# Hybrid GLA / RG-LRU block on one core: output weights split beside the attention, second gate on the results

## The chip, the cores and the metric

The kernel runs on one NeuronCore of a Trainium2 chip. The engines are named as the profile names them: PE (TensorE, matmuls), DVE (VectorE), ACT (ScalarE), POOL (GpSimd), SP (SyncE, which issues most of the DMA transfers; POOL issues some). The metric is the time of one execution on the device, in microseconds; less is better.

## What is computed

The reference takes 1024 latent tokens and 256 context tokens of width 1024 (1280 rows, ten tiles of 128) through two layers. Layer 0 has gated linear attention with four heads and, beside it, a short gated convolution; layer 1 has a gated linear recurrence in both directions. Cut to what matters here:

```python
# layer 0 (x and the context alike)
h = rmsnorm(x) * (1 + scale) + shift
q, k, v, g_a, a_f, a_b, c_b, c_c, c_x, g_b = split(h @ w_in)
o = rmsnorm(gla_fwd(q, k, v, a_f) + gla_bwd(q, k, v, a_b)) * silu(g_a)
y = c_b * conv3(c_c * c_x) * silu(g_b)
x = x + gate0 * (concat(o, y) @ w_out0)        # w_out0: 2048 x 1024
# layer 1
h = rmsnorm(x) * (1 + scale1) + shift1
y = (rglru_fwd(h @ w_x) + rglru_bwd(h @ w_x)) * silu(h @ w_g)
x = x + gate1 * (y @ w_out1)                   # w_out1: 2048 x 1024
return rmsnorm(x) * final_g
```

`gate0` and `gate1` are rows of 1024 numbers, one for each column of the result.

## The kernel before

All is float32, and the matmuls keep that precision by parts: each operand is split into a rounded part `hi` and a rest `lo`, and `mm3` (L125 to L127) makes three matmuls of a product, hi x hi, hi x lo and lo x hi. Activations of a layer stand split in `hhi` and `hlo`. A weight tile is 128 x 512 numbers, 256 KB. `load_split` (L106 to L112) brings one in: a transfer on SP's queue into one of two `raw` buffers, a cast to `hi` on ACT (L111), and a subtraction for `lo` on DVE (L112), into one of six `hl` buffers that all weights share. A unit of projection weights is two such tiles (1024 x 128 weights) and gives PE 72 matmuls, 24 products over columns 256, 512 and 512.

Layer 0 goes head by head. For each of four heads `emit_gla` is written first, the attention proper: small float32 matmuls (`pz`, `psc`, `pk`, `pst`, `po`, `pot`) that hang on long chains over ACT and DVE. Then come two gate units (`wgt`), the conv channel's units `cc`, `cx`, `cb` and its gate unit, and then q, k and v of the next head. Their projections need nothing but their weights, and the scheduler of the framework mixes the attention's matmuls in between them; it decides each engine's order when the program is built, and on the chip each engine keeps it.

Between these units stands `presplit` (L166): layer 1's input weights are split while layer 0 runs. One call for one tile is a load into `raw` (L106), cast, subtraction, and two stores of 256 KB each (L173) into `w1s_d` in DRAM, all on SP's queue. There are 80 tiles, five at each of four points of a head. In layer 1 `load_parts` (L178) brings both parts back with one transfer of 512 KB on POOL's queue, with no cast.

The output projections are `out_group` (L632). Layer 0's runs over three groups of row tiles (3, 3 and 4 tiles), layer 1's over two of 4. Each group loops over 16 slices k of the inner dimension and two halves j of the columns, and every (k, j) needs one tile of the output weight: 32 tiles a group, 96 loads in layer 0 and 64 in layer 1, each by `load_split` (`rawo`, `wo`). The gated activations y come by SP's queue as well. The products of the last two slices are held back and done row tile by row tile. What the results are multiplied with differs: layer 0 and layer 1's first group multiply the results in PSUM by the gate row and add the residual; layer 1's second group has the gate in its weights (`gate=gb1`, one more DVE operation for each tile, L110) and only adds the residual (L978).

POOL has little to do besides the transfers of parts: the powers of the norms, `rr` (L90), one for each row tile.

## Time and profile before

| | us |
|---|---|
| median of 3 runs | 1995.36 (1992.71 to 1997.35) |
| the profiled execution | 2002.68 |
| its span on the core | 2000.9 |
| PE busy in the span | 1932.0 |
| DVE, ACT, POOL busy | 1317.8, 961.3, 105.2 |

In the span, the four heads of layer 0's attention take about 90 to 783 us, the other conv channels go on to about 960, layer 0's output projection runs from 985 to about 1272, the recurrence of layer 1 follows, and layer 1's output projection ends the kernel from about 1780. Engine names with a q (SPq) are that engine's queue of instructions. The view of busy time by stretch has, for each stretch in us from the span's start, its length, the busy time of each engine with its number of instructions, the granted share of PE's clock (1.00 is 2.4 GHz), the busy share of the 16 transfer engines, and GB/s. The view of one tile gives for each line, engine and operation the count, the shortest, median and longest duration in ns, and the first and last start in us. The timeline gives start and duration in us, and in brackets how long the engine was idle and what released it.

### The profile page before, as it was taken

What the parts mean: (1) busy time and instruction counts of PE and PEld (TensorE: products, weight loads), DVE (VectorE), ACT (ScalarE), POOL (GpSimd) and SP (SyncE); (2) the same over time, 40 slices, a digit from 0 to 9 for tenths busy, and PEclk for the clock granted to TensorE, in tenths of its full rate; (3) what the DMA queues carried; (4) which work ended last, traced back from release to release, by engine and by line L of the source; (5) the groups of instructions that cost most, each with busy time, mean ns of one, the idle gap of its engine ahead of it and who ended that gap; (6) DMA issues with size and microseconds to landing.
All of it is one profiled execution on the core that took longest, in us unless ns stands there. A gap on an engine that the chain in (4) does not pass through costs nothing.

```text
span 2000.9 us, 27096 instructions
## 1 busy us (share of the span) xinstructions
PE 1932.0 (97%) x9884; PEld 1588.5 (79%) x9884; DVE 1317.8 (66%) x2103; ACT 961.3 (48%) x1690; POOL 105.2 (5%) x154
## 2 busy tenths in 40 slices
PE   9899999999999999999999899999999999998988
PEld 5777898888788888888776678878888888876767
DVE  6746436543552554388557474689999999996595
ACT  4333344334433433311345444267777776876452
POOL 1000000000000000000000000201111010100000
PEclk9999999999999999999999999999999999999999
DMA  9256217514721751366655665434333343324782
GB/s 357 82 195 199 78 50 252 175 43 146 244 89 33 245 192 53 124 223 197 205 175 178 209 222 173 139 111 127 120 118 120 115 121 121 116 81 156 264 290 88
DMA packets 162522, 311.45 MB, mean 156 GB/s; under 512 B 16338, under 2 KB 37202, under 8 KB 162260
## 3 DMA queue, kind: packets, MB, share of 16 engines
q1 hardware_dynamic: 140628, 267.78, 40.1%
q0 software_dynamic: 21760, 41.95, 7.5%
q8 instruction: 77, 1.26, 0.3%
q14 instruction: 57, 0.47, 0.1%
HBM read 221.05 MB, written 88.60 MB: 155 GB/s over the span
## 4 chain that ended last, share of the span: by engine, by line
PE 60%; DMA 19%; DVE 12%; ACT 5%; issue 4%; SPq 1%; POOL 0%; DVEq 0%; ACTq 0%; POOLq 0%
PE pjgt L126 4%; PE pjgt L127 4%; PE pjgt L125 4%; DMA rawpre<-in_w1f 4%; PE pjxr L125 4%; PE pjxr L127 4%; PE pjxr L126 4%; PE pO L126 3%; PE pO L125 3%; PE pO L127 3%; PE po L515 2%; DMA wt<-in_wmT 2%; DMA rawo<-in_w0out 2%; PE pv L125 2%; PE pv L126 2%
## 5 line engine op out<-in xcount | busy, mean ns | idle before, releaser
L125 PE MATMUL pjgt<-hhi,wgt 128*128 128x512 f32 (+1 forms) x640 | 240.6, 376 | 6.0 <-DVE zc L218 6.0
L125 PE MATMUL pO<-wo,yh 128*128 128x512 f32 x576 | 224.2, 405 | 17.6 <-ACT wo L111 16.6
L126 PE MATMUL pjgt<-hlo,wgt 128*128 128x512 f32 (+1 forms) x640 | 240.5, 376 | 0.0
L127 PE MATMUL pjgt<-hhi,wgt 128*128 128x512 f32 (+1 forms) x640 | 239.5, 376 | 0.0
L126 PE MATMUL pO<-wo,yh 128*128 128x512 f32 x576 | 231.1, 402 | 7.2 <-DVE wo L112 7.2
L127 PE MATMUL pO<-wo,yl 128*128 128x512 f32 x576 | 228.5, 399 | 0.0
L806 DVE SCALAR_TENSOR_TENSOR xc<-xp,col,xc 128x1283 f32<-128x1283 f32 (+2 forms) x102 | 149.8, 1476 | 3.2
L111 ACT CAST wo<-rawo 128x512 fp32r<-128x512 f32 x160 | 98.0, 619 | 110.7 <-DMA rawo<-in_w0out 74.9
L112 DVE TENSOR_TENSOR wo<-rawo,wo 128x512 fp32r<-128x512 f32 x160 | 108.5, 687 | 63.6 <-ACT wo L111 63.0
L125 PEld LDWEIGHTS pO<-wo,yh 128*128 128x128 f32 x576 | 109.3, 191 | 50.0 <-ACT wo L111 22.5
L125 PEld LDWEIGHTS pjgt<-hhi,wgt 128*128 128x128 f32 x640 | 121.0, 189 | 30.1 <-DVE zc L218 6.6
L126 PEld LDWEIGHTS pjgt<-hlo,wgt 128*128 128x128 f32 x640 | 121.1, 189 | 23.7 <-issue 1.1
L127 PEld LDWEIGHTS pjgt<-hhi,wgt 128*128 128x128 f32 x640 | 120.5, 189 | 23.4 <-issue 0.7
L126 PEld LDWEIGHTS pO<-wo,yh 128*128 128x128 f32 x576 | 109.7, 190 | 36.8 <-DVE wo L112 12.4
L125 PE MATMUL pjxr<-hhi,wxr 128*128 128x512 f32 (+1 forms) x384 | 137.4, 359 | 0.0
L126 PE MATMUL pjxr<-hlo,wxr 128*128 128x512 f32 (+1 forms) x384 | 137.1, 358 | 0.0
L127 PE MATMUL pjxr<-hhi,wxr 128*128 128x512 f32 (+1 forms) x384 | 136.8, 358 | 0.0
L127 PEld LDWEIGHTS pO<-wo,yl 128*128 128x128 f32 x576 | 109.8, 191 | 24.6 <-DVE yl L685 0.3
L112 DVE TENSOR_TENSOR wpre<-rawpre,wpre 128x512 fp32r<-128x512 f32 x80 | 55.1, 690 | 90.1 <-ACT wpre L111 89.7
L125 PE MATMUL pv<-wv,hhi 128*128 128x256 f32 (+1 forms) x320 | 91.8, 287 | 2.4 <-ACT v L387 2.4
L127 PE MATMUL pv<-wv,hlo 128*128 128x256 f32 (+1 forms) x320 | 92.9, 290 | 0.0
L126 PE MATMUL pv<-wv,hhi 128*128 128x256 f32 (+1 forms) x320 | 92.8, 290 | 0.0
(270 smaller groups left out, 4527.9 us busy)
## 6 DMA issues: line engine op xcount, KB each, us to landing
w1s_d<-wpre SPq DMA_DIRECT2D x160, 256.0 KB, 2.6
rawo<-in_w0out SPq DMA_DIRECT2D x96, 256.0 KB, 3.2
rawpre<-in_w1f SPq DMA_DIRECT2D x64, 256.0 KB, 3.1
wt<-in_wmT SPq DMA_DIRECT2D x32, 512.0 KB, 4.3
rawo<-in_w1out SPq DMA_DIRECT2D x64, 256.0 KB, 3.3
wxr<-w1s_d POOLq DMA_DIRECT2D x32, 512.0 KB, 3.8
wgt<-w1s_d POOLq DMA_DIRECT2D x32, 512.0 KB, 3.8
wm<-in_wmT SPq DMA_DIRECT2D x24, 512.0 KB, 8.1
```

Source lines behind the costliest of these rows:

```text
L111: S.copy(hi, raw)
L112: V.tensor_tensor(lo, raw, hi.bitcast(F32), ALU.subtract)
L125: PE.matmul(ps, a[0], b[0], start=first, stop=False)
L126: PE.matmul(ps, a[0], b[1], start=False, stop=False)
L127: PE.matmul(ps, a[1], b[0], start=False, stop=last)
L515: PE.matmul(ps[:, :DV], l, r, start=(i == 0), stop=(i == len(pairs) - 1))
L806: V.scalar_tensor_tensor(x, tap(j), cw[j], x, op0=ALU.mult, op1=ALU.add)
```

## The change

It does three things. The 64 tiles of both output weights (32 each) are put at the head of the list that `presplit` works through, and each of the four points of a head takes nine tiles instead of five. Their parts go to `wos_d`, one such tensor for each layer. `out_group` and `load_w1` then load parts: one transfer of 512 KB on POOL's queue for each tile, straight into an `hl` buffer (6 of them, or 8 of its own pool in layer 1's second group), no cast, no subtraction. And since these parts have no gate in them, layer 1's second group multiplies its results by the gate row as the first one does.

```diff
-    todo = [(b, j) for b in range(NB) for j in range(5)]
+    wos_d = [dram.tile([32, P, 2, 512], F32, name=f"wos{l}_d") for l in range(2)]
+    todo = [(l, k, j, None) for l in range(2) for k in range(16) for j in range(2)]
+    todo += [(b, j) for b in range(NB) for j in range(5)]
...
-            b, j = todo.pop(0)
+            b, j, *o = todo.pop(0)
+            if o:
+                hi, lo = load_split((w0out, w1out)[b][j, :, 512 * o[0]:512 * o[0] + 512], 512,
+                                    f"preo{b}_{j}_{o[0]}", queue=SY.dma_start)
+                for i, part in enumerate((hi, lo)):
+                    SY.dma_start(wos_d[b][2 * j + o[0]][:, i], part.bitcast(F32))
+                continue
...
                 emit_raw_gate(w0f[8 + 2 * h], 2 * h)
-                presplit(5)
+                presplit(9)
                 emit_raw_gate(w0f[9 + 2 * h], 2 * h + 1)
-                presplit(5)
+                presplit(9)
                 for _ in emit_conv(h):
-                    presplit(5)
+                    presplit(9)
...
         def load_w(k, j):
+            if parts is not None:
+                pool, n = (wkw["pool"], 8) if wkw else (wpool, 6)
+                hl = pool.tile([P, 2, 512 if n == 8 else UW], F32R, tag="hl", bufs=n, name=f"wo{name}{g0}_{k}_{j}")
+                G.dma_start(hl[:, :, :512], parts[2 * k + j])
+                return hl[:, 0, :512], hl[:, 1, :512]
...
-            w1[k, j] = load_split(w1out[k, :, j * 512:(j + 1) * 512], 512, f"o10_{k}_{j}")
+            hl = wpool.tile([P, 2, UW], F32R, tag="hl", bufs=6, name=f"wo10_{k}_{j}")[:, :, :512]
+            G.dma_start(hl, wos_d[1][2 * k + j])
+            w1[k, j] = hl[:, 0], hl[:, 1]
...
-                                                 gate=gb1, late_k=3, pool=op, bufs=(4, 8), width=512)
+                                                 late_k=3, pool=op, parts=wos_d[1])
...
-                    if g0:
-                        V.tensor_tensor(x2[:, fs], acc[i][j], xr[:, fs], ALU.add)
-                    else:
-                        V.tensor_tensor(x2[:, fs], acc[i][j], gb1[:, fs], ALU.mult)
-                        V.tensor_tensor(x2[:, fs], x2[:, fs], xr[:, fs], ALU.add)
+                    V.tensor_tensor(x2[:, fs], acc[i][j], gb1[:, fs], ALU.mult)
+                    V.tensor_tensor(x2[:, fs], x2[:, fs], xr[:, fs], ALU.add)
```

How the order of instructions moves. On SP's queue, in the second head, between the last load for `cx` and the loads for `cb`, there stood before five pre-splits (`rawpre` is a load, `w1s_d<-wpre` the two stores of one):

```order
L97 DMA rawcx_0_1_3869<-in_w0f 128x512
L106 DMA rawpre_0_3957<-in_w1f 128x512
L106 DMA rawpre_1_3964<-in_w1f 128x512
L173 DMA w1s_d<-wpre_0_3959 128x512 x2
L106 DMA rawpre_2_3971<-in_w1ax 128x512
L173 DMA w1s_d<-wpre_1_3966 128x512 x2
L106 DMA rawpre_3_3978<-in_w1f 128x512
L173 DMA w1s_d<-wpre_2_3973 128x512 x2
L106 DMA rawpre_4_3985<-in_w1f 128x512
L173 DMA w1s_d<-wpre_3_3980 128x512 x2
L97 DMA rawcb_0_0_3992<-in_w0f 128x512
```

Now nine stand there, all of layer 1's output weight; these are the last five of them (`rawpreo` is a load, `wos_d<-wpreo` the two stores of one):

```order
L106 DMA rawpreo_13_0_4155<-in_w1out 128x512
L176 DMA wos_d<-wpreo_12_1_4150 128x512 x2
L106 DMA rawpreo_13_1_4162<-in_w1out 128x512
L176 DMA wos_d<-wpreo_13_0_4157 128x512 x2
L106 DMA rawpreo_14_0_4169<-in_w1out 128x512
L176 DMA wos_d<-wpreo_13_1_4164 128x512 x2
L106 DMA rawpreo_14_1_4176<-in_w1out 128x512
L176 DMA wos_d<-wpreo_14_0_4171 128x512 x2
L106 DMA rawpreo_15_0_4183<-in_w1out 128x512
L176 DMA wos_d<-wpreo_14_1_4178 128x512 x2
L97 DMA rawcb_0_0_4190<-in_w0f 128x512
```

The load for `cb` has moved behind four more loads and eight more stores; the same holds at each of the four points of each head.

On PE, in the same head, the rows just ahead of the first product with `cc`'s weights were, before, the end of the second gate unit (`pjgt`) and the attention's transposes and scores of the first of the two 512-row chunks that the backward pass takes (`pk`, `psc`, named 768):

```order
L465 MATMUL pk_1_768_3038<-ident,k_1_1_768_3024 128x128 x4
L488 MATMUL psc_1_6_3044<-qh_1_768_3022,kh_1_768_3023 64x128
L489 MATMUL psc_1_6_3044<-qh_1_768_3022,kh_1_768_3023 64x64
L127 MATMUL pjgt_768_3711<-hhi,wgt_0_1_3652 128x512
L125 MATMUL pjgt_768_3711<-hhi,wgt_0_1_3652 128x512
L126 MATMUL pjgt_768_3711<-hlo,wgt_0_1_3652 128x512
L127 MATMUL pjgt_768_3711<-hhi,wgt_0_1_3652 128x512
L125 MATMUL pjcc_0_3786<-hhi,wcc_0_0_3778 128x256
```

Now the scores of the next chunk (named 256) stand there as well, and the state products `pst` of the first chunk lie ahead of them:

```order
L497 MATMUL psc_1_2_3228<-qh_1_256_3206,kh_1_256_3207 64x128
L498 MATMUL psc_1_2_3228<-qh_1_256_3206,kh_1_256_3207 64x64
L497 MATMUL psc_1_2_3228<-qh_1_256_3206,kh_1_256_3207 64x128
L498 MATMUL psc_1_2_3228<-qh_1_256_3206,kh_1_256_3207 64x64
L497 MATMUL psc_1_2_3228<-qh_1_256_3206,kh_1_256_3207 64x128
L498 MATMUL psc_1_2_3228<-qh_1_256_3206,kh_1_256_3207 64x64
L497 MATMUL psc_1_2_3228<-qh_1_256_3206,kh_1_256_3207 64x128
L498 MATMUL psc_1_2_3228<-qh_1_256_3206,kh_1_256_3207 64x64
L474 MATMUL pk_1_256_3222<-ident,k_1_1_256_3208 128x128 x4
L125 MATMUL pjcc_0_3956<-hhi,wcc_0_0_3948 128x256
```

From the head's first gate product to this place, the attention's matmuls have grown from 12 psc, 6 pk, 2 pst and 1 pz to 20, 10, 6 and 2; up to the conv channel's gate unit from 20 psc, 10 pk, 9 pst, 3 pz and no po or pot to 32, 16, 13, 4, 12 and 6.

On POOL's queue, at the end of layer 0's first group of row tiles, only the powers of the norms stood before:

```order
L90 TENSOR_TENSOR rro_9_6981<-rvo_9_6979,m_77 128x1
L90 TENSOR_TENSOR rr_0_10051<-rv_0_10049,m_77 128x1
L90 TENSOR_TENSOR rr_1_10065<-rv_1_10063,m_77 128x1
L90 TENSOR_TENSOR rr_2_10080<-rv_2_10078,m_77 128x1
L90 TENSOR_TENSOR rr_3_10880<-rv_3_10878,m_77 128x1
```

Now the loads of the next group's weights stand ahead of them, each of which waits for a free `hl` buffer:

```order
L654 DMA wo_15_0_10277<-wos_d 128x2x512
L654 DMA wo_15_1_10279<-wos_d 128x2x512
L654 DMA wo_0_0_10549<-wos_d 128x2x512
L654 DMA wo_0_1_10560<-wos_d 128x2x512
L654 DMA wo_1_0_10581<-wos_d 128x2x512
L90 TENSOR_TENSOR rr_0_10405<-rv_0_10403,m_77 128x1
L90 TENSOR_TENSOR rr_1_10419<-rv_1_10417,m_77 128x1
L654 DMA wo_1_1_10592<-wos_d 128x2x512
L654 DMA wo_2_0_10613<-wos_d 128x2x512
L654 DMA wo_2_1_10624<-wos_d 128x2x512
L90 TENSOR_TENSOR rr_2_10434<-rv_2_10432,m_77 128x1
```

The powers of a group's rows have moved behind three to six loads for the group after it.

## Rows read from the trace of the kernel before

**Rows 1.** The page's busy table: PE's busy us, share and instructions, whole span.

```profile
PE 1932.0 (97%) x9884; PEld 1588.5 (79%) x9884; DVE 1317.8 (66%) x2103; ACT 961.3 (48%) x1690; POOL 105.2 (5%) x154
```

**Rows 2.** Busy time by stretch: a head's pre-splits, output of layer 0, output of layer 1.

```profile
296.00:373.00 77.00, 76.69 (x423) 62.91 (x422) 45.82 (x93) 35.20 (x79) 0.00 (x0) 1.00 0.75 249
985.00:1272.00 287.00, 270.92 (x1189) 212.58 (x1189) 166.37 (x309) 129.42 (x235) 14.99 (x15) 0.99 0.61 191
1780.00:1994.00 214.00, 198.03 (x820) 155.06 (x818) 151.29 (x232) 109.06 (x183) 5.02 (x7) 0.97 0.56 190
```

**Rows 3.** PE's waits, 985 to 1280 us: total us, times, longest us.

```profile
PE pO L125 <- ACT wo L111: 5.1, 4, 1.8
PE pO L126 <- DVE wo L112: 3.3, 7, 1.0
```

**Rows 4.** PE's waits, 1780 to 2001 us.

```profile
PE pO L125 <- ACT wo L111: 11.5, 8, 2.5
PE pO L126 <- DVE wo L112: 3.9, 4, 2.0
```

**Rows 5.** View of tile wpre, second head (296 to 373 us): its subtractions.

```profile
L112 DVE TENSOR_TENSOR wpre<-rawpre,wpre x20: 676/692/695, 296.7 to 369.3; 128x512 fp32r<-128x512 f32 x20
```

**Rows 6.** Timeline of SP's queue in the third run of that head.

```profile
341.50 0.45 SPq L106 DMA_DIRECT2D rawpre<-in_w1ax  x1
...
346.27 0.41 SPq L106 DMA_DIRECT2D rawpre<-in_w1f  x1
```

**Rows 7.** Tile wpre by stretch: DVE, ACT busy, clock, transfer share, GB/s; two runs.

```profile
316.30:329.10 12.80, 3.41 (x5) 2.46 (x4) 1.00 0.91 306
340.40:351.60 11.20, 3.45 (x5) 2.49 (x4) 1.00 0.90 298
```

**Rows 8.** Views of tiles wcc, wcb, wgt in that head: casts and first products.

```profile
L111 ACT CAST wcc<-rawcc x2: 619/619/619, 330.6 to 333.6; 128x512 fp32r<-128x512 f32 x2
L125 PE MATMUL pjcc<-hhi,wcc x24: 278/395/585, 331.3 to 347.1; 128*128 128x512 f32 x16, 128*128 128x256 f32 x8
L111 ACT CAST wcb<-rawcb x2: 620/620/620, 353.0 to 355.9; 128x512 fp32r<-128x512 f32 x2
L125 PE MATMUL pjcb<-hhi,wcb x24: 277/395/397, 365.5 to 378.8; 128*128 128x512 f32 x16, 128*128 128x256 f32 x8
L111 ACT CAST wgt<-rawgt x2: 622/624/625, 371.2 to 373.6; 128x512 fp32r<-128x512 f32 x2
L125 PE MATMUL pjgt<-hhi,wgt x24: 277/395/582, 379.5 to 397.5; 128*128 128x512 f32 x16, 128*128 128x256 f32 x8
```

**Rows 9.** Timeline of PE, attention products between gate products (two instructions each).

```profile
308.11 0.32 PE L488 MATMUL psc<-qh,kh 128*64 128x128 f32 x1
...
308.88 0.48 PE L127 MATMUL pjgt<-hhi,wgt 128*128 128x512 f32 x1
...
313.38 1.02 PE L504 MATMUL pst<-v,k1T 128*128 128x256 f32 x4
314.34 0.50 PE L411 MATMUL pz<-aT,wst 64*128 64x512 f32 x1
314.77 0.39 PE L125 MATMUL pjgt<-hhi,wgt 128*128 128x256 f32 x1
```

**Rows 10.** The chain that ended last: three po, six instructions; start and us.

```profile
239.36 1.29 PE po L515 x6
```

**Rows 11.** Timeline of PE, the first head's first product with cc's weights.

```profile
149.71 0.50 PE L125 MATMUL pjcc<-hhi,wcc 128*128 128x256 f32 x1 [4.19 <-ACT wcc L111]
```

**Rows 12.** Busy time by stretch just behind it.

```profile
150.00:154.00 4.00, 4.00 (x25) 2.98 (x25) 2.31 (x6) 0.41 (x2) 0.00 (x0) 0.59 0.39 104
```

**Rows 13.** The page's queues: packets, MB, share of 16 engines (q1 SP, q0 POOL).

```profile
q1 hardware_dynamic: 140628, 267.78, 40.1%
q0 software_dynamic: 21760, 41.95, 7.5%
```

**Rows 14.** Timeline of DVE at the kernel's end: the last results' addition.

```profile
1993.92 0.69 DVE L978 TENSOR_TENSOR x<-pO,xr 128x512 f32<-128x512 f32 x1
```

More of the change, by code (lines that the diff above doesn't have):

```diff
@@ L630, in hybrid_kernel, with out_group @@
     BANKS = "AAAGGGBB"
-    def out_group(g0, gn, nk, get_y, wsrc, name, hooks={}, gate=None, late_k=2, ahead={}, **wkw):
+    def out_group(g0, gn, nk, get_y, wsrc, name, hooks={}, gate=None, late_k=2, ahead={}, parts=None, **wkw):
         acc = [[bank(BANKS[2 * i + j], f"pO{name}{g0}_{i}_{j}") for j in range(2)] for i in range(gn)]
@@ L704, in get_y @@
                              C("glag", k % 2) if k < 2 * H else None, pool, bufs)
-            acc = out_group(g0, gn, 2 * KD, get_y, w0out, "0")
+            acc = out_group(g0, gn, 2 * KD, get_y, w0out, "0", parts=wos_d[0])
             if g0 == 0:
@@ L955, in hybrid_kernel @@
         acc1 = out_group(0, 4, NB, lambda k: y1.pop((0, k), None) or y1_gated(0, k), w1out, "1", hooks,
-                         ahead=w1)
+                         ahead=w1, parts=wos_d[1])
     h_scope.close()
```

## The prediction

> **What bounds the kernel now.** I read the busy table first, then the busy time by stretch, then who waited for whom in the two output stages, and last, for one attention head, when each weight tile is ready and when TensorE first uses it. TensorE (PE) is busy 1932.0 of 2000.9 us [rows 1], and it takes its instructions in program order, so the time changes only where PE waits longer or less. In the stretch of an attention head that carries the pre-splits, PE is busy 76.69 of 77.00 us [rows 2]: there is no idle time to win there, and none to hide a wait in. The output projection of layer 0 (985 to 1272 us) has 16.1 us of idle PE, that of layer 1 (1780 to 1994) 16.0 us [rows 2]. Of these, PE waited 5.1 + 3.3 = 8.4 us for a split of an output weight (cast L111, subtraction L112) in layer 0 [rows 3], and 11.5 + 3.9 = 15.4 us in layer 1 [rows 4]. So the change can win some 24 us of waits at the two output stages, and what it moves goes into the one place where PE is full.
>
> **What the change moves into attention, and its price.** 64 tiles of output weight join the 80 pre-splits, so each head has 36 instead of 20: nine instead of five at each of four points (ahead of the second gate unit's weights, ahead of cc, ahead of cb, ahead of the conv channel's gate unit). On SP's queue they stand ahead of these weights, one behind the other, as the order rows of cx to cb show: five pairs of load and stores before, nine now.
>
> How long does one pre-split hold up the queue? In the second head 20 of them and 8 halves of unit weights pass DVE from 296.7 to 369.3 us [rows 5]: 27 steps in 72.6 us, 2.69 us each. Two raw buffers set this pace: the load of 341.50 and the load two pre-splits later, of 346.27, are 4.77 us apart [rows 6], 2.39 us for one at best; within the runs of five the steps are (12.80 - 0.69)/4 = 3.03 us and (11.20 - 0.69)/4 = 2.63 us by the lengths of [rows 7]. A pre-split moves 0.79 MB (256 KB in, 512 KB out), and in these runs the transfer engines are already 0.91 and 0.90 busy at 306 and 298 GB/s [rows 7], which by itself allows one in about 2.35 us. I take 2.7 us, the mean of the whole stretch, with 2.4 and 3.0 as ends. Longer runs can't go much faster, because the transfer engines are nearly full.
>
> Now the lead of each weight [rows 8], counted at its first cast. cc: cast from 330.6, finished some 331.2, first used at 331.3: no lead at all. cb: finished at 353.6, used at 365.5: lead 11.9 us. The conv channel's gate: finished at 371.8, used at 379.5: lead 7.7 us. Ahead of cc stand 8 more pre-splits, ahead of cb 12, ahead of that gate 16. They delay the weights by 8 x 2.7 = 21.6, 32.4 and 43.2 us.
>
> What else could PE do in that time? Only what now stands ahead of cc in its order. The order rows show it: the scheduler has pulled attention products forward, in the second head 8 psc, 4 pk, 4 pst and one pz. From the timeline 4 psc with 2 pk take 308.11 to 308.88 = 0.77 us, 2 pst 313.38 to 314.34 = 0.96 us, a pz 0.43 us [rows 9]: 1.5 + 1.9 + 0.4 = 3.9 us in all. So PE waits 21.6 - 3.9 = 17.7 us for the second gate's and cc's weights together. For cb nothing more: PE comes 17.7 + about 7 us later and has 11.9 us of lead, together 37 against 32.4. For the gate of the conv channel: by then some 11 us of attention work in total have been pulled forward (12 psc, 6 pk, 4 pst, one pz, 12 po at 1.29/3 = 0.43 us [rows 10], 6 pot, taken as a pk each), so PE comes 17.7 + 11 = 28.7 us later and had 7.7: it waits 43.2 - 36.4 = 6.8 us. Behind it q, k and v have time. A head loses 17.7 + 6.8 = 24.5 us, four heads 98 us. With 2.4 us for a pre-split it is 15.3 + 3.7 = 19.0 a head, 76 in all; with 3.0 us it is 20.1 + 9.2 = 29.3, 117 in all.
>
> **The clock.** In the first head PE waited 4.19 us for cc [rows 11], and the granted clock of the 4 us from 150 is 0.59 [rows 12], half the time or more at 1.2 instead of 2.4 GHz: 0.41 x 4 = 1.6 us lost. After the waits for the second gate and cc a slow start costs little, since the next weights are late anyway; only after the last wait of a head is nothing late behind it. I take 4 x 1.6 = 6 us, from 0 to 12. The Trainium skill (TensorE: Matmul & The Clock Gate, section on HAM oscillation) says that the array is throttled again at each such gap and pays for it each time. By that rule alone the three gaps of a head would all count, an estimate of 12 x 1.6 = 20 us instead of 6; this trace shows one such gap in attention, and no row with a late weight behind it.
>
> **What it takes out of the output stages.** Layer 0: 96 loads of 256 KB with their cast and subtraction go, 96 loads of 512 KB on POOL's queue come, with nothing between landing and use. The waits of 8.4 us are at stake. But the bytes double: the transfer engines are 0.61 busy in these 287 us [rows 2], 175 us. The 25.2 MB that go moved at 267.78 MB/(0.401 x 2000.9 us) = 334 GB/s, 75 us; the 50.3 MB that come move at the rate of POOL's queue, 41.95/(0.075 x 2000.9) = 280 GB/s [rows 13], 180 us. That is 280 us of transfer in a stage of 287, with six tiles of look-ahead: waits for casts become waits for transfers. I take 0, from -10 (all of 8.4 and the clock that goes with it) to +20. Layer 1: 214 us at 0.56 [rows 2] are 120 us of transfer; 16.8 MB leave (50 us), 33.6 MB come (120 us), 190 of 214. That still fits, and DVE no longer multiplies the second group's weights by the gate. I take -10 of 15.4, from -22 (all, and two slow starts of the clock) to 0. The gate on the results adds one DVE operation of 0.69 us behind the last matmul [rows 14]: +1. Where POOL's order now has weights ahead of the norm's powers (rr), these wait for a weight buffer; PE has the next group's first matmuls meanwhile, so I count nothing, and up to 5 us within the +20.
>
> **The sum.** 98 + 6 + 0 - 10 + 1 = +95 us. The profiled execution took 2002.68 us (span 2000.9), the median of three runs is 1995.36; the sum is put on the median: 2090 us. Ends: 76 + 0 - 10 - 22 + 1 = +45 (2040) and 117 + 12 + 20 + 0 + 1 = +150 (2145).
>
> **Rivals.**
> (a) Faster: the pre-splits hide, the output stages win 10 to 32 us, about 1975. This needs PE to have 21.6 us of other work ahead of cc in each head. Attention products are the only work that needs no weight, and a head has some 30 us of them; but they hang on chains over ACT and DVE, and the order brings only 3.9 us forward. It decides where the added delay stays under 3.9 us, 0.5 us a pre-split; the shortest step seen is 2.39. 5%.
> (b) One wait instead of two: cc stalls PE, and PE then comes so late that the gate's weights are there, because the products pulled forward take longer than I priced: 4 x 17.7 = 71, + 6 - 10 + 1: about 2063. For it: the products wait on ACT and DVE, which now hold more casts in order. Within the range. 20%.
> (c) Output stages starve as well: layer 0 at +20 on top of slow pre-splits, 2125 to 2160. For it: 280 of 287 us of transfer, and bursts of loads at the groups' ends. 13%.
> (d) The change doesn't do what it says, in that one gain or cost cancels the other within 0.2%: the attention waits would have to stay under 14 us in four heads. 3%.
> My own case (2075 to 2115): 57%; the rest, 2%, lies between 2000 and 2040.
>
> **How the numbers follow.** Likeliest 2090. The range takes the ends of the sum, 2040 to 2140; left out are (a), (d), the 2% and about half of (c), 16 to 17 in 100. Faster by over 0.2% (about what a measurement of this kernel can tell from no change): 0.05; within 0.2%: 0.03; slower: 0.92.
>
> **What would show it.** In the profile after, each head should be some 24 us longer; PE should wait for the cast of wgt and wcc some 18 us a head and for wgt of the conv channel some 7; the granted clock should fall below full speed several times between 130 and 900 us; pre-splits should come in runs of nine at 2.4 to 3 us. In the output stages no wait for a cast of wo, but waits for wo<-wos_d in layer 0, with the transfer engines over 0.9 busy. The forecast is wrong if PE is still full in the heads: then the pre-splits go faster than any row of before shows, or PE has found more work than the order shows.

## The result and the profile after

The changed kernel takes 2109.69 us (median of four runs, 2102.36 to 2111.42) against 1996.36 us (1992.71 to 1998.42) for the kernel before on the same chip: ratio 1.0563, 95% interval 1.0533 to 1.0593. It is slower, as forecast (2090, range 2040 to 2140). The profiled execution of after took 2102.36 us, its span is 2099.8 us.

The page's busy table of after answers to [rows 1]: PE has the same 9884 matmuls, but they take 20 us longer, and the span has 148 us without one, where there were 69.

```profile
PE 1951.8 (93%) x9884; PEld 1610.0 (77%) x9884; DVE 1246.3 (59%) x1983; ACT 903.2 (43%) x1594; POOL 211.9 (10%) x314
```

Stages are read from the timeline of PE: attention and conv channels run from the last row tile of V in the first head to the first product with layer 0's output weights, each output group from its first such product to its last. In us of the profiled executions:

| stage | before | after | difference | predicted |
|---|---|---|---|---|
| attention and conv channels | 871.7 | 986.4 | +114.7 | +104 |
| output of layer 0, three groups | 280.8 | 268.5 | -12.3 | 0 |
| output of layer 1, first group | 102.3 | 110.3 | +8.0 | -10 with the next row |
| output of layer 1, second group | 100.5 | 87.2 | -13.3 | |
| from the last matmul to the end | 7.0 | 9.7 | +2.7 | +1 |
| span | 2000.9 | 2099.8 | +98.9 | +95 |

The view of busy time by stretch shows the second head, from V to V, of before and then of after (columns as in [rows 2]):

```profile
297.80:475.00 177.20, 175.73 (x1036) 149.56 (x1035) 84.61 (x183) 72.76 (x176) 5.47 (x10) 1.00 0.43 142
```
```profile
324.50:534.10 209.60, 183.69 (x1037) 154.62 (x1035) 94.30 (x199) 81.54 (x192) 5.49 (x10) 0.93 0.53 180
```

The head is 32.4 us longer: PE idles 25.9 us instead of 1.5, and the same matmuls take 8 us more, because the granted clock of the head is 0.93. Over the whole stage PE's busy time grows from 854.7 to 882.9 us. So of the 114.7 us, 86.5 are waits and 28.2 are slower matmuls. The trace's record of the granted clock bears that out: in this stage PE is busy for 66.6 us at the lower of its two levels (1.2 GHz instead of 2.4), before for 9.0 us. Half of the difference, 28.8 us, is an estimate of what that cost.

PE's waits from 90 to 900 us, in the view of waits of after (all but 2.2 us of the whole stage's):

```profile
PE pjgt L125 <- ACT wgt L111: 35.0, 5, 10.0
PE psc L497 <- DVE kh L465: 20.4, 4, 8.7
PE pjcc L125 <- ACT wcc L111: 16.5, 3, 12.9
PE po L524 <- DVE Cs L508: 11.7, 4, 3.6
PE psc L493 <- DVE kh L465: 6.2, 2, 4.3
PE pot L531 <- ACT on L528: 5.7, 3, 4.0
```

The casts that the prediction named stand there, wgt and wcc with 51.5 us, but as much again (kh, Cs, on and smaller ones) is for operands of the attention products, which ACT and DVE make. Before, the same view of that stretch has 0.8 us for kh and no row for Cs or on. By place, from PE's timeline (us, in the four heads; the last row has the rest of the stage as well):

| PE idle | before | after | more | predicted |
|---|---|---|---|---|
| first gate unit to the first product of cc | 4.7 | 71.8 | +67.1 | +71 |
| from there to the conv channel's gate unit | 2.5 | 29.4 | +26.9 | +27 |
| whole stage | 17.0 | 103.5 | +86.5 | +98 |

Ahead of cc, 50.9 us are for the weights of the second gate unit and of cc, and 20.4 us for kh. Behind it only 0.6 us are for the gate's weights; the rest is for attention operands.

Why these come late can be read ahead of the longest wait for kh, in the last head (timelines of ACT, DVE and PE). ACT takes its instructions in order and stands still for the loads of two pre-splits, and kh is made behind their casts:

```profile
784.98 0.62 ACT L111 CAST wpre<-rawpre 128x512 fp32r<-128x512 f32 x1 [2.55 <-DMA rawpre<-in_w1f]
791.04 0.62 ACT L111 CAST wpre<-rawpre 128x512 fp32r<-128x512 f32 x1 [1.89 <-DMA rawpre<-in_w1f]
791.88 0.40 ACT L462 ACTIVATE kh<-b 128x256 f32<-128x256 f32 x1
793.98 0.69 DVE L465 TENSOR_TENSOR kh<-kh,k 128x512 f32<-128x512 f32 x1
794.72 0.47 PE L497 MATMUL psc<-qh,kh 128*64 128x128 f32 x1 [8.70 <-DVE kh L465]
```

What waits do to the clock, in the first head: a wait for weights (timeline of PE) with the stretch around it, and a stretch with waits of 4.31 us for kh and 2.15 us for Cs (the clock is the last column but two):

```profile
137.85 0.58 PE L125 MATMUL pjgt<-hhi,wgt 128*128 128x256 f32 x1 [6.44 <-ACT wgt L111]
```
```profile
135.00:142.00 7.00, 4.15 (x15) 3.77 (x16) 5.87 (x15) 3.71 (x10) 0.00 (x0) 0.51 0.55 186
225.00:240.00 15.00, 8.37 (x36) 6.41 (x37) 10.81 (x24) 6.52 (x17) 0.55 (x1) 0.66 0.81 280
```

In the output stages the casts are gone, as said. Layer 0's stage (1099 to 1368 us) has PE's wait for parts at 1.2 us in all, although the transfers are 0.91 busy:

```profile
PE pO L125 <- DMA wo<-wos_d: 1.2, 1, 1.2
```
```profile
1099.00:1368.00 269.00, 262.09 (x1154) 210.16 (x1153) 106.02 (x212) 73.52 (x140) 73.09 (x103) 0.99 0.91 284
```

Layer 1's first group has one long wait. The timeline of PE shows it, and the timeline of POOL's queue what stands ahead of these loads: eight loads for the second group, which has buffers of its own, go out from 1953.5 to 1964, ahead of the first group's last six, of which the first is issued at 1965.99 (the bracket gives what POOL waited for).

```profile
1983.86 0.77 PE L125 MATMUL pO<-wo,yh 128*128 128x512 f32 x1 [13.84 <-DMA wo<-wos_d]
```
```profile
1953.53 3.92 POOL L654 DMA_DIRECT2D wo<-wos_d  x7 [2.08 <-PE pO L127]
1958.46 0.54 POOL L654 DMA_DIRECT2D wo<-wos_d  x1 [1.00 <-DMA wo<-wos_d]
1963.78 0.53 POOL L654 DMA_DIRECT2D wo<-wos_d  x1 [4.79 <-DMA wo<-wos_d]
1965.99 0.71 POOL L654 DMA_DIRECT2D wo<-wos_d  x1 [1.67 <-DMA wo<-wos_d]
```

At the end DVE has the gate's multiplication between the last matmul and the addition, and the row tile before gets its norm applied (1.42 us) in between: the tail grows by 2.7 us, not by one operation ([rows 14]).

```profile
2090.64 0.68 DVE L993 TENSOR_TENSOR x<-pO,gb 128x512 f32<-128x512 f32 x1
2091.45 1.42 DVE L999 SCALAR_TENSOR_TENSOR x<-x,rr,fg 128x512 f32<-128x512 f32 x2
2092.78 0.68 DVE L994 TENSOR_TENSOR x<-x,xr 128x512 f32<-128x512 f32 x1
```

### The profile page after: what moved, and what is told of

It is laid out like the page before. It is cut to its first block, busy times and chain, and to the rows that moved or that the text cites. A ratio compares the mean times of both kernels' runs of the same rounds, so it can differ in the third digit from the quotient of the medians.

```text
span 2099.8 us, 27172 instructions
## 1 busy us (share of the span) xinstructions
PE 1951.8 (93%) x9884; PEld 1610.0 (77%) x9884; DVE 1246.3 (59%) x1983; ACT 903.2 (43%) x1594; POOL 211.9 (10%) x314
## 3 DMA queue, kind: packets, MB, share of 16 engines
q0 software_dynamic: 61184, 125.84, 20.0%
## 4 chain that ended last, share of the span: by engine, by line
PE 62%; DMA 20%; DVE 9%; ACT 4%; issue 4%; SPq 1%; POOL 0%; ACTq 0%; DVEq 0%; POOLq 0%
PE pO L125 5%; PE pO L126 5%; PE pO L127 5%; DMA rawpre<-in_w1f 5%; PE pjgt L125 4%; PE pjgt L126 4%; PE pjgt L127 4%; PE pjxr L127 4%; PE pjxr L125 4%; PE pjxr L126 4%; DMA rawpreo<-in_w0out 3%; PE po L524 2%; DMA wt<-in_wmT 2%; DMA rawpreo<-in_w1out 2%; PE pv L127 2%
## 5 line engine op out<-in xcount | busy, mean ns | idle before, releaser
L125 PE MATMUL pjgt<-hhi,wgt 128*128 128x512 f32 (+1 forms) x640 | 245.0, 383 | 37.3 <-ACT wgt L111 35.0
L125 PE MATMUL pO<-wo,yh 128*128 128x512 f32 x576 | 230.3, 401 | 18.3 <-DMA wo<-wos_d 15.0
L127 PE MATMUL pjgt<-hhi,wgt 128*128 128x512 f32 (+1 forms) x640 | 240.1, 379 | 0.0
L126 PE MATMUL pO<-wo,yh 128*128 128x512 f32 x576 | 230.2, 400 | 0.0
L654 POOL DMA_DIRECT2D wo<-wos_d x158 | 107.8, 683 | 510.2 <-PE pO L127 259.3
L699 DVE TENSOR_TENSOR yl<-y,yh 128x512 fp32r<-128x512 f32 (+1 forms) x80 | 50.7, 636 | 103.8 <-ACT yh L698 103.8
L698 ACT CAST yh<-y 128x512 fp32r<-128x512 f32 (+1 forms) x80 | 45.6, 574 | 153.5 <-PE pO L126 98.6
L682 ACT ACTIVATE ga<-ga 128x512 f32<-128x512 f32 (+1 forms) x80 | 46.9, 588 | 135.3 <-DMA ga<-gt_d 104.9
L90 POOL TENSOR_TENSOR rro<-rvo,m 128x1 f32<-128x1 f32 x40 | 22.0, 549 | 819.8 <-DVE rvo L88 819.8
```

The lines of the kernel that those rows point to most:

```text
L90: G.tensor_tensor(r, v, m05, ALU.pow)
L125: PE.matmul(ps, a[0], b[0], start=first, stop=False)
L126: PE.matmul(ps, a[0], b[1], start=False, stop=False)
L127: PE.matmul(ps, a[1], b[0], start=False, stop=last)
L654: G.dma_start(hl[:, :, :512], parts[2 * k + j])
L682: silu = S.activation(ga, ga, AF.Silu)
```

## Taking the change apart

Ratios are to the kernel before, run on the same chip; stages are of the profiled executions. Of each edit the lines that matter are shown, and `...` stands for lines left out.

**Pre-splits alone.** Nine at a point and their stores, the output stages as before:

```diff
-            acc = out_group(g0, gn, 2 * KD, get_y, w0out, "0", parts=wos_d[0])
+            acc = out_group(g0, gn, 2 * KD, get_y, w0out, "0")
...
```

> The changed kernel's 36 pre-splits a head, with their stores into wos_d, but both output projections as in the kernel before: weights loaded and split there, the second group's gate in its weights. The stored parts of the output weights are not read. Theory: the whole loss comes from the pre-splits that stand ahead of the weights in the attention, where the trace after is 115 us longer in four heads; so about 1996 + 115 = 2111 us (2095 to 2125), heads as long as after, output stages as long as before (281 and 210 us from the first product to the last). By the prediction's own sum for the attention (98 + 6) it would be 2100. Rival: a part of the loss comes with the reading of the parts (512 KB transfers, POOL's queue). Then the time is under 2085 and the heads are shorter than after.

Measured: 2125.91 us, 1.0627 (1.0604 to 1.0650); attention +125.0 us, layer 0's output 280.3 us, layer 1's groups 103.7 and 100.8. The median lies just over the expected 2095 to 2125. The whole loss comes from the pre-splits. That the stage is ten us longer than in the changed kernel needs no further cause: the profiled executions lie 26 us apart, but the kernels by their two ratios only 13, about the 15 us that the changed kernel wins behind the attention.

**Parts alone.** The other half, with the 20 pre-splits a head of before:

```diff
-    wos_d = [dram.tile([32, P, 2, 512], F32, name=f"wos{l}_d") for l in range(2)]
+    wos_d = [w1s_d[32 * l:32 * l + 32] for l in range(2)]
...
-                presplit(9)
+                presplit(5)
...
```

> The output stages of the changed kernel alone: parts by POOL's queue, gate on the results, but only the 20 pre-splits a head of the kernel before. It reads parts of layer 1's input weights in place of those of the output weights, so the numbers that come out are others, the work is the same. Theory: the output stages win what the trace after shows, 12 us in layer 0 and 3 in layer 1 with its tail: 1996 - 15 = 1981 us (1975 to 1987). The prediction's sum (0, -10, +1) gives 1987. Rival: layer 0's gain in the trace after comes only because the attention ends late, for instance by a clock that recovers; then layer 0 takes 281 us here too and the time is about 1993.

Measured: 1992.71 us, 0.9963 (0.9945 to 0.9980). Layer 0's output takes 272.1 us (-8.7), layer 1's groups 109.0 and 87.2. The median misses the expected 1975 to 1987 and is the rival's 1993, but the rival's reason falls: layer 0's stage is shorter without a longer attention. By the median the gain is 7 us, the prediction's size rather than the trace's 15. The size of layer 0's part is uncertain: its stage takes 276 to 281 us in the four profiled executions with the code of before, and 268 to 276 us in the eight that read parts with the six buffers of before, so the gain is some 7 us on average.

**The gate on the results alone.**

```diff
-                                                 gate=gb1, late_k=3, pool=op, bufs=(4, 8), width=512)
+                                                 late_k=3, pool=op, bufs=(4, 8), width=512)
...
-                    if g0:
-                        V.tensor_tensor(x2[:, fs], acc[i][j], xr[:, fs], ALU.add)
...
```

> The kernel before, with one part of the change: layer 1's second group takes its gate on the results. Nothing is pre-split beyond the 80 tiles. Theory: 32 multiplications of 0.69 us leave the chain from the load of a weight to its product, where PE waited for casts; this gives a part of the 13 us by which the second group was shorter after, against 2.7 us at the tail: -4 us, from -9 to +1. Rival: the waits were for the loads, not for DVE; then only the tail is left, +2 to +3 us.

Measured: 1990.36 us, 0.9950 (0.9933 to 0.9968). The second group takes 87.2 us, as long as with parts: the gate alone gives all of its gain, and the pre-split weights add nothing to it. The median is 9.5 us under before, at the far end of the expected -9 to +1.

**The order on POOL's queue.** Parts alone, with the second group's loads tied behind the first group's:

```diff
+                if n == 8:
+                    tc.add_manual_dep(d.ins, last_part[0], mybir.DependencyInfo(
+                        mybir.DependencyClass.NoSync, mybir.DependencyReason.DATA), reason="load order")
...
```

> The parts-alone kernel (0.9963 of the kernel before; first group of layer 1's output projection 109 us, against 102 before), with one thing changed: on POOL's queue the second group's loads stand behind the first group's last six, where eight of them stood ahead. It reads parts of other weights, as that kernel does. Theory: the single wait of some 14 us for wo in the first group goes: group 109 to 96-101 us, total 8 to 13 us under the parts-alone kernel, 0.990 to 0.993 of before. Rival: the transfers of that stretch are full anyway (residual rows, gate row and 8 MB of parts at once), and the wait moves to the second group's first weights: the same total within 3 us.

Measured: 0.9934 (0.9919 to 0.9949). The first group takes 95.2 us instead of 109.0, the second 90.6 instead of 87.2. PE's wait for wo is gone from the view of waits, whose longest row there is now

```profile
PE pO L125 <- ACT yh L703: 3.6, 2, 3.5
```

So the order was the cause of that wait: 3.4 us of the 13.8 come back as a slower second group. The total moved 6 us by the ratios, less than the 8 expected and more than the rival's 3; the intervals of the two ratios just touch.

## Why a pre-split delays the weights

**Without the raw buffers.** The forecast held that the transfers, 0.9 busy, leave no faster pace than 2.35 us. In this kernel the load goes into the hl buffer's second half, where lo will stand:

```diff
...
+        if queue is not load:
+            raw = lo.bitcast(F32)
+            queue(raw, src)
```

> The changed kernel, but a pre-split needs no raw buffer: its load goes into the half of the hl buffer that lo will take, and the subtraction is done in place. Six hl buffers stay. Theory of the prediction: two raw buffers set the pace of 2.7 us; without them it falls to what the transfers allow, 2.35 us, so 27 pre-splits ahead of the last weight of a head are 9 us earlier, and the time is about 2109 - 4 x 9 = 2073 us (2060 to 2085), runs of nine at 2.4 us. Rival: the transfers themselves set the pace (0.79 MB each, transfer engines 0.9 busy): the same 2.6 to 2.8 us a pre-split and the same 2105 to 2113 us.

Measured: 2020.90 us, 1.0108 (1.0086 to 1.0130), with the same 144 pre-splits and the same bytes: some 90 us less than the changed kernel, where at most 50 were expected. Attention is +29.7 us instead of +114.7. The first eight pre-splits of the second head pass DVE from 306.0 to 320.5 us, 2.0 us from one to the next, where the changed kernel's runs of nine have 2.8 to 3.5 us. And the transfers move more than the forecast thought they could:

```profile
306.10:320.50 14.40, 14.40 (x76) 11.46 (x75) 9.64 (x24) 7.82 (x21) 0.00 (x0) 1.00 0.97 341
327.20:345.30 18.10, 13.38 (x71) 10.04 (x70) 13.76 (x28) 11.26 (x24) 0.00 (x0) 0.97 1.00 364
```

The trace of before showed as much, ahead of the attention:

```profile
25.00:50.00 25.00, 22.88 (x140) 16.28 (x140) 20.85 (x53) 10.90 (x18) 3.02 (x5) 1.00 1.01 389
```

The waits for attention operands shrink as well, though the casts are the same: PE waits some 10 us for kh, on and smaller ones, instead of some 50. That fits slow loads, and not the casts as such, as what makes them late.

The timeline of SP's queue tells the pace. First the changed kernel: with two raw buffers, loads go out by twos, and the next two wait until the casts and subtractions of these are done, 5.8 to 6.4 us a pair.

```profile
113.74 0.96 SPq L106 DMA_DIRECT2D rawpreo<-in_w0out  x2
118.11 1.96 SPq L176 DMA_DIRECT2D wos_d<-wpreo  x4
120.17 0.91 SPq L106 DMA_DIRECT2D rawpreo<-in_w0out  x2
123.80 2.05 SPq L176 DMA_DIRECT2D wos_d<-wpreo  x4
125.95 0.91 SPq L106 DMA_DIRECT2D rawpreo<-in_w0out  x2
```

In place the six hl buffers let up to four loads go out together, with six or eight stores between:

```profile
303.99 1.03 SPq L112 DMA_DIRECT2D wpreo<-in_w1out  x2
305.98 3.96 SPq L180 DMA_DIRECT2D wos_d<-wpreo  x6
311.74 3.58 SPq L112 DMA_DIRECT2D wpreo<-in_w1out  x4
317.06 4.78 SPq L180 DMA_DIRECT2D wos_d<-wpreo  x8
```

**Is in-place better by itself?** The kernel before, with only the edit of the in-place kernel:

```diff
...
+            raw = lo.bitcast(F32)
+            queue(raw, src)
```

> The kernel before with nothing but the in-place pre-splits, 20 a head. Theory: with five at a point the two raw buffers cost little, since PE waited only some 11 us in the four heads and the weights came just in time: -3 us (-8 to +1). Rival: in-place pre-splits are better than raw ones by an amount of their own (some 0.8 us each, as between the changed kernel and its in-place form: 89 us for 144); then 80 of them give -30 us or more, and the gain of the in-place run says nothing on the added ones.

Measured: 1994.57 us, 0.9991 (0.9973 to 1.0009), attention -0.4 us. Five at a point cost nothing either way, so the 90 us belong to the added ones.

**How many fit?** Only layer 0's 32 tiles are added, seven at a point, in place, with the gate on the results:

```diff
+    todo = [(0, k, j, None) for k in range(16) for j in range(2)]
...
-                presplit(9)
+                presplit(7)
...
```

> Pre-splits without a raw buffer, as in the in-place run, but only layer 0's 32 output tiles are added (seven pre-splits at each point instead of nine). Layer 1's output weights are loaded and split there as before, its second group takes the gate on the results. Theory: what is left of the loss in the heads (37 us with 16 more pre-splits a head, in place) goes with their number, so 18 us with eight more; layer 0's output stage wins 12, the gate on the results 10: about 1996 + 18 - 12 - 10 = 1992 us. Rival: the loss has a threshold, because the weights of before had leads of 8 to 12 us; then eight more cost next to nothing and the time is about 1976.

Measured: 1981.82 us, 0.9934 (0.9920 to 0.9949), attention -0.2 us: the eight added ones a head cost nothing, where 16 cost 30 us. So there is a threshold in place, as the rival had it. The same kernel with the two raw buffers of before:

```diff
...
-            raw = lo.bitcast(F32)
-            queue(raw, src)
+        raw = pool.tile([P, width], F32, tag="raw", bufs=bufs[0], name=f"raw{name}")[:, :n]
+        queue(raw, src)
```

> The seven-a-point kernel (layer 0's 32 output tiles added, gate on the results) with the two raw buffers of the changed kernel instead of the in-place subtraction. Theory: n pre-splits and the two tiles of the next unit must pass while PE works on one unit (16.4 us for 72 matmuls). Five at 2.7 us and two tiles at some 1.25 us are 16.0 us, just under it; seven are 21.4 us, 5 us over, at the points ahead of the second gate unit and of cc; attention products fill some 4 of these 10. So 6 to 10 us a head, 25 to 40 in all: 1982 + 32 = 2014 us (2005 to 2025). By the prediction's own sum (cc delayed by 4 x 2.7 less 3.9 us) it is 28 us, 2010. Rival: the loss goes with the number of added tiles, half of the changed kernel's 115: 2039. Second rival: the raw buffers matter only with nine; then 1985.

Measured: 2025.78 us, 1.0173 (1.0158 to 1.0187), attention +43.3 us. That is over the expected 25 to 40 and under the proportional loss of 57; by the two ratios the raw buffers cost 48 us, nearer to the proportional loss than to the middle of the forecast. So with raw buffers a threshold isn't shown. And in place with eight at a point (the last 16 tiles are not read):

```diff
...
-                presplit(7)
+                presplit(8)
```

> The seven-a-point in-place kernel (0.9934 of before) with eight at a point: 16 more tiles, of layer 1's output weight, are split and stored but not read. Theory: in place a pre-split takes some 1.85 us, so eight and two tiles are 17.3 us against the 16.4 us of a unit, 0.9 over at two to four points of a head: 7 to 15 us in all, 1989 to 1997 us. With nine it was 2.8 us over, and 37 us. Rival: there is no threshold, and the loss of 37 us with nine came with layer 1's tiles as such; then eight cost nothing, 1982.

Measured: 1974.58 us, 0.9922 (0.9902 to 0.9941), attention -12.6 us. Eight still fit, where I expected 7 to 15 us of loss. The rival expected this, with layer 1's tiles as such as the reason of the loss with nine. That reason falls by the trace of the in-place kernel with nine: its four heads lose 8.2, 8.6, 8.9 and 4.0 us, and the last two carry none of these tiles, so the number at a point counts. Timed, seven and eight can't be told apart; why the profiled attention is 12 us shorter with eight stays open (it takes 868.8 to 872.0 us in the four kernels that leave it as it was). Its second head has no idle PE at all:

```profile
292.30:468.70 176.40, 176.40 (x1037) 149.67 (x1035) 92.00 (x194) 78.24 (x188) 5.48 (x10) 1.00 0.58 196
```

Its weights come just in time (tile wcb in that head: last subtraction from 358.8 to 359.5 us, first product at 359.9). The attention stage by pre-splits at a point, in us against before:

| at a point | two raw buffers | in place |
|---|---|---|
| 5 | 0 | -0.4 |
| 7 | +43.3 | -0.2 |
| 8 | | -12.6 |
| 9 | +114.7 | +29.7 |

One unit of weights gives PE 16.5 us of work (second gate unit to cc, 314.8 to 331.3 before). My account was that the pre-splits of a point and two weight tiles have to pass in that time. It is an estimate, and the runs don't bear out its numbers: five at 2.7 us with two tiles are about 16 us and free, but eight in place, some 2 us apart, are 18 us with two tiles, and free as well. That in place the edge lies between eight and nine is shown; why it lies there is not. Past it the 16 tiles more cost 30 us against seven at a point and 42 against eight, 1.9 or 2.6 us each. With raw buffers the first 32 tiles added cost 1.4 us each, the next 32 cost 2.2 us each.

**Buffers of their own.** In place the pre-splits of a head start only when PE leaves V (first subtraction at 306.0, V's last row tile at 304.4 us), since the six buffers go round with the weights'. Here they have two of their own and the weights four:

```diff
+        mine = split if split_ring[0] else next(turns) % 6 >= 4
+        if mine:
+            return wpool.tile([P, 2, 512], F32R, tag="hp", bufs=2, name=name)
+        return wpool.tile([P, 2, UW], F32R, tag="hl", bufs=4, name=name)
...
```

> The changed kernel with all 144 pre-splits, in place, and with two buffers of their own for the length of the attention; the weights there keep four. Elsewhere six as before. Theory: in the in-place run a head's pre-splits begin only when PE has left the four tiles of V (first subtraction at 306.0 us, V's last row tile at 304.4), since they share the six buffers in turn with the weights; with their own they go beside V, where transfers are few, and the heads become as long as before: 2109 - 115 = 1995 us (1985 to 2003). Rival: what is left in the heads comes from the casts in ACT's and DVE's order or from the transfers; then it stays at 2015 to 2025, or is worse, since two buffers give one pre-split in some 3 us and four buffers give the weights less lead.

Measured: 2071.44 us, 1.0377 (1.0354 to 1.0401). My theory fell, and the rival's "or is worse" came. With two buffers the pace is slow again, although in place: 13 pre-splits from 285.3 to 329.8 us, 3.7 us apart, at a transfer share of 0.68. That is one more sign that the number of buffers sets it. The pre-splits do run beside V, and most weights come 11 to 20 us early, yet the first two heads are 26 and 35 us longer than before. PE now waits for ACT and DVE, in the view of waits of these two heads:

```profile
PE pot L544 <- ACT on L541: 8.4, 5, 3.0
PE psc L506 <- DVE kh L478: 8.3, 3, 4.6
PE pv L138 <- ACT v L409: 6.5, 4, 4.0
PE psc L510 <- DVE kh L478: 5.4, 2, 3.4
```

and ACT, in the same stretch, for the loads of pre-splits, some 180 us in all:

```profile
ACT wpre L124 <- DMA wpre<-in_w1f: 78.6, 30, 4.9
ACT wpreo L124 <- DMA wpreo<-in_w1out: 60.1, 25, 4.8
ACT wpreo L124 <- DMA wpreo<-in_w0out: 26.8, 10, 4.0
```

**The same without the added casts.** What is loaded is stored as both parts:

```diff
...
+                raw = new_hl(f"wpreo{b}_{j}_{o[0]}", True)[:, 1].bitcast(F32)
...
+                for i in range(2):
+                    SY.dma_start(wos_d[b][2 * j + o[0]][:, i], raw)
```

> The own-ring kernel (2071 us), with the same loads and stores, but the 64 added tiles are neither cast nor subtracted: what was loaded is stored as both parts, so the output projections compute with other weights. The 80 tiles of layer 1's input weights keep their casts. In the own-ring run the weights were early (leads of 11 to 20 us) and yet the first two heads, which carry nearly all of the added tiles, were 28 us longer each than before. Theory: ACT and DVE take their instructions in order and wait there for a pre-split's load, so that the attention's products come late; without these casts the first two heads fall to some 180 us each and the time to 2071 - 50 = 2020 us (2010 to 2030). Rival: it is the transfers or SP's queue, which stay as they are: 2060 to 2075.

Measured: 2037.01 us, 1.0231 (1.0216 to 1.0246), by the ratios 29 us less than with them, between the expected 50 and the rival's nothing. The first head falls from 209.7 to 201.3 us, the second from 212.3 to 198.9; before they took 183.8 and 177.2. So the added casts are a part of the cost of this kernel, 22 of the 61 us in these heads. That this is ACT's and DVE's order alone isn't shown: without the casts the stores on SP's queue no longer wait for ACT either (55.7 us in these heads with them), and the transfers of the first head rise from 0.68 to 0.78 busy. The other part stays open: the second head still has eight pre-splits with casts, and the queue and the transfers (0.78 busy in the first head) were not told apart.

**Another place.** In place, layer 0's 32 tiles beside the conv channels behind the attention:

```diff
...
+        presplit(4)
+        for _ in emit_conv(ct):
+            presplit(4)
...
```

> In place; the attention carries only the 80 tiles of before, five at each point; layer 0's 32 output tiles are split beside the four conv channels after the attention (four ahead of each channel, and four at each of its two points). Layer 1 as before but for the gate on the results. Theory: the weights of these channels have a lead of some 37 us, so eight to twelve pre-splits at under 2.7 us a channel are hidden: heads as before, layer 0's output stage -12, gate on the results -10: about 1974 us (1966 to 1985), faster than both kernels. Rival: the stretch from 783 to 985 us already loads 16.8 MB of modulation weights and the last channels then wait for weights: 5 to 20 us longer there, 1980 to 1995.

Measured: 2000.25 us, 1.0024 (1.0013 to 1.0035). The heads are as short as in the other in-place kernels, but the conv channels and the modulation end 19 us later. One wait stands for half of it: PE waits for the gate row, whose modulation weights (`wt`) come by the same queue.

```profile
PE pggate L641 <- DVE dggate L640: 10.9, 2, 10.6
```

The rival expected such waits, with 5 to 20 us and a time of 1980 to 1995; the time is over that too. The weights' lead of 37 us there was no sign that the queue had room.

## Why the prediction was right, and where not

- **Direction and size.** The sum of +95 us stands against +98.9 between the profiled executions. The medians differ by 113, since the profiled execution of before lies 6 us over its median and that of after 7 us under; putting the sum on the median lost those 14 us. That the sum came so near is in part luck: the clock was 22 us over its term, the waits 12 and the output stages with the tail 6 under theirs. A slip besides: with 2.4 us for a pre-split the formula for the gate's wait gives 4.4 us and not 3.7, so the low end of the waits is 79 us and not 76, which moves the range by 3 us.
- **Pace of a pre-split.** 2.7 us was nearly right: counted as in the prediction, over pre-splits and halves of weights, a step takes 2.8 to 2.9 us in the four heads of after; within the runs of nine it is 2.8 to 3.5 us, over the forecast 2.4 to 3. The reason beside it was half wrong. That two raw buffers set it is shown by the in-place kernel, and the one with two buffers of its own, slow again, fits it. That the transfers, 0.91 busy at 306 GB/s [rows 7], allow no less than 2.35 us is refuted by 2.0 us at 341 to 364 GB/s.
- **Waits in the heads.** 98 us predicted, 86.5 measured. Place by place the sizes fit, 67 us ahead of cc against 71 and 27 behind it against 27. What PE waited for does not: the sign that it would wait some 7 us a head for the conv channel's gate failed (0.6 us in all four), and of the waits ahead of cc 20 us were for kh. The step that failed is the one that priced attention products as free filling of 3.9 and 11 us: they are made by ACT and DVE, whose order now has more casts that wait for loads, and PE waited some 50 us for them. While it did, weights came in that it would have waited for instead, so the two errors offset each other.
- **Clock.** 6 us (0 to 12) predicted, 28.2 measured as longer matmuls: the term that was mis-sized most. I let only the last wait of a head count, but the granted clock fell again and again, to 0.51 and 0.66 in the stretches above and 0.93 over the heads. How much of the 28.2 us made the stage longer is not shown: with faster matmuls PE might have waited longer for the same weights, as the prediction argued. The rule of the Trainium skill (TensorE: Matmul & The Clock Gate, section on HAM oscillation), that each such gap is paid for, gave 20 us and was the better guide to the matmuls' time; this trace agrees with its direction.
- **Output of layer 0.** 0 predicted, -12.3 in the trace of after, -8.7 with parts alone; it lies two us outside the stated ends in the one and inside in the other. The failing step is the 280 of 287 us of transfer, which took the 280 GB/s of POOL's queue [rows 13] for its limit. The transfers were busy 0.91 of 269 us, 245 us, and PE waited 1.2 us for parts. So "waits for casts become waits for transfers" was wrong here.
- **Output of layer 1.** -10 predicted, -5.3 measured, for other reasons. The gate on the results gives -13.3, and the parts cost +7 to +8 through the order on POOL's queue; in order they win 7. That later loads stand ahead on this queue was seen for the powers in layer 0, and not looked for in layer 1.
- **Rivals.** (a) needed pre-splits under 0.5 us each; the in-place kernels show that it is decided otherwise, since seven and eight at a point cost nothing there at some 2 us each. (b) came true in its mechanism, though not in its time of 2063: PE came so late to the conv channel's gate that its weights were there, because the attention products took longer than priced, waiting for ACT and DVE. What (b) overlooked is that this lateness costs as much as the wait that it replaces. (c) didn't come, since layer 0's output won. (d) was far off.

**A version that beats both** is the one with seven in place for layer 0 alone and the gate on the results: 1981.82 us, 0.9934 of before, 0.940 of after by the two ratios. The kernel with eight has 0.9922, which can't be told from it. Most of that gain may be the gate's: on the results alone it has 0.9950, and the intervals overlap, so what the pre-splits of layer 0 add is not clear of the noise.

## What to carry to other kernels

Background work on a shared in-order queue can be free up to a threshold and dear past it, here between eight and nine pre-splits at a point in place: what is queued between two needed loads delays the second one. Count the buffers before the bytes when you price its pace: two staging buffers, not the transfers, set it here. Where the work also puts casts on other engines, they wait in order for its loads, and the work that those engines feed becomes late as well. And price a wait by place: which of two late inputs ends it may change without changing its length.

## What I had not expected of the hardware

- A busy share of 0.9 of the transfer engines is not a limit: 306 GB/s at 0.91 [rows 7], 341 at 0.97 and 364 at 1.00 in place, 389 at 1.01 at the start of before.
- POOL's queue moved 280 GB/s over the kernel before [rows 13] and, in after, a mean of 125.84 MB/(0.200 x 2099.8 us) = 300 GB/s:

```profile
q0 software_dynamic: 61184, 125.84, 20.0%
```

- The clock's price: the same matmuls of the attention stage took 28.2 us longer in after (882.9 against 854.7 us busy), with heads at 0.93 of the granted clock where they had 0.99 to 1.00.
